# Output projections: the first token group stores its split weights to memory, and the later groups load them instead of splitting again

## The chip, the cores and the metric

The kernel runs on one core of one Trainium2 chip. The metric is the device time of one execution in microseconds (us). The engines are named as in the profile: PE (TensorE, matmuls), DVE (VectorE), ACT (ScalarE), POOL (GpSimd) and SP (SyncE, which here does little but issue transfers; SPq is its queue). "L298" is line 298 of the kernel.

## What is computed

The reference is a backbone of two layers over 1024 latent tokens and 256 context tokens, with a width of 1024. The change touches the last matrix product of each layer's token mixer, `@ w_out`:

```python
# layer 0 (mixer_ab): all 1024 latent tokens and the 256 context tokens
y_l = jnp.concatenate([a_l, b_l], axis=-1) @ w_out      # w_out: 1024 x 1024
y_c = jnp.concatenate([a_c, b_c], axis=-1) @ w_out
# layer 1 (mixer_cd): the latent tokens only, since the context is not needed behind the last layer
y_l = jnp.concatenate([c_l, d_l], axis=-1) @ w_out
...
xl = xl + ml[:, :, 2] * rms_norm(yl, g[1])
hl = modulate(rms_norm(xl, g[2]), ml[:, :, 3], ml[:, :, 4])
xl = xl + ml[:, :, 5] * rms_norm(conv_glu_ffn(hl, ...), g[3])
```

The products are made in float32 precision out of three faster ones: each operand is split into a rounded high part and a low remainder, and a product is high x high + low x high + high x low.

## The kernel before

**Tiles.** The tokens are worked in three groups: group 0 and group 1 of 512 latent tokens, and group 2, the context, of 256 (`TOK`). `outproj` (L588) makes one group's projection out of eight column tiles `o` of the weight, each 128 columns wide. For each tile `wcol` (L303) loads 128x8x128 floats of the weight (`wr`, 512 KB, L290), ACT rounds it to the high part `wh` (L295), and DVE or POOL subtracts to get the low part `wl` (L298): POOL throughout the projection of layer 0, DVE throughout that of layer 1. Then `gemm` issues 24 matmuls (L315 to L317: for each of 8 slices of the contraction one with `wh` and the input's high part, one with `wh` and its low part, one with `wl`). ACT copies the result out of the accumulator to `ys[o]` and squares it, and POOL adds the squares up (L472) for the norm.

Every group loads and splits the same eight tiles anew: three times in layer 0, twice in layer 1.

**Buffers.** `wr` has two buffers, so raw tiles are loaded ahead. `wh` and `wl` come from a pool `wgp` of two buffers each; in layer 0 every third tile goes to a third buffer in another pool (`third`, L302 to L306).

**What runs beside it.** `update` (L523) of a group starts when the group's projection is done, and works while the next one's matmuls run: it loads the residual x from memory (`xd`, L560), norms y (`rstd_y`: PE adds the squares over partitions at L436, `ones,sq`; DVE finds the reciprocal root in some twelve small steps at L439 to L444; DVE builds a diagonal matrix `dg` at L451, and PE spreads it at L456, `dg,ones`), adds y to x (DVE, L513 and L514), stores x (L547), squares it (ACT L468, POOL L472) and norms it for the FFN (DVE L495 and L498, ACT `hh`, POOL `hl` L502). `cat.load` of the next group loads and norms part of its input (`cln`, L812 to L841; its outputs are `cch` and `ccl`). After the projections the FFN starts: its first tile is two half tiles (`big`) for groups 0 and 1, and needs the normed x of both.

**What sets the order.** Instructions of an engine run in the order of its program. That order is made when the kernel is built, by flows that are advanced by estimated work (`pump`, and the numbers in `yield`), and then by a scheduler. All transfers of this stretch go through SP's queue in program order: a transfer that waits for a buffer or for data holds up all those behind it.

The same store and load of split weights is there already for another matrix: the FFN's down weights of layer 0 are stored to `wdd` (L1540) and loaded for the context (L1596).

Of the kernel before, what the change touches and what calls it, by code (L numbers as in the profile page):

```python
# [11 lines left out]
F32 = mybir.dt.float32  # L12
F32R = mybir.dt.float32r
# [60 lines left out]
PO1 = (), ("n+++++nn",)  # L74
PO0 = (), (), ()
# [15 lines left out]
OR0 = ()  # L91
GO0 = 0, 1, 2
YPO = 0, 1
U2 = 0, 1
PU1 = (), ("n+++++nn",)


@with_exitstack
def tile_backbone(ctx: ExitStack, tc: tile.TileContext, a: dict, out: bass.AP):
    nc = tc.nc  # L100
# [6 lines left out]
    wgp = ctx.enter_context(tc.tile_pool(name="wgp", bufs=2))  # L107
# [11 lines left out]
    drp = ctx.enter_context(tc.tile_pool(name="drp", bufs=1, space=DRAM))  # L119
# [3 lines left out]
    def nm(s):  # L123
        uid[0] += 1
        return f"{s}{uid[0]}"
# [5 lines left out]
    def psum_side(key, n):  # L131
        psy[0].close()
        psy[0] = ExitStack()
        psum[key] = psy[0].enter_context(tc.tile_pool(name=nm(key), bufs=n, space=PSUM))
# [8 lines left out]
    def page(shape, dt=F32, s="pg"):  # L143
        return pgp.tile(shape, dt, tag="pg", name=nm(s))
# [25 lines left out]
    def spawn(gen, key="norm"):  # L170
        flows.setdefault(key, deque()).append([gen, 0.0])
# [26 lines left out]
    def bank():  # L198
        return psum["mm"].tile([128, 512], F32, tag="mm", name=nm("mm"))
# [10 lines left out]
    def acts(g, n, dt=F32, s="act"):  # L210
        w = 2 if g < 2 else 4
        res = []
        for i in range(0, n, w):
            p = page([128, w, TOK[g]], dt, s)
            res += [p[:, j] for j in range(min(w, n - i))]
        return res
# [10 lines left out]
    def f32(ap):  # L227
        return ap.bitcast(F32)
# [59 lines left out]
    def load_w(src, nk, m=128):  # L288
        raw = rawp[0].tile([128, 8, 128], F32, tag="wr", name=nm("wr"), **({} if rawp[0] is wrp else {"bufs": 3}))
        nc.sync.dma_start(raw[:, 0:nk, 0:m], src)  # L290
        return raw

    def split_w(raw, nk=8, m=128, pages=False, pool=None, **kw):
        hi, lo = (page([128, 8, 128], F32R, x) if pages else (pool or wgp).tile([128, 8, 128], F32R, tag=x, name=nm(x), **kw) for x in ("wh", "wl"))
        S.copy(hi[:, 0:nk, 0:m], raw[:, 0:nk, 0:m])  # L295
        e = WS[ws[0]]
        wn[0] += 1
        (G if e[wn[0] % len(e)] == "G" else V).tensor_sub(lo[:, 0:nk, 0:m], raw[:, 0:nk, 0:m], f32(hi[:, 0:nk, 0:m]))  # L298
        return hi, lo
# [3 lines left out]
    def wcol(w, c0, m=128, pool=None, **kw):  # L303
        third[1] += 1
        if third[0] and third[1] % 3 == 0:
            pool, kw = ph[0], {"bufs": third[0]}  # L306
        nk = w.shape[0] // 128
        return split_w(load_w(w[:, c0:c0 + m].rearrange("(k p) m -> p k m", p=128), nk, m), nk, m, pool=pool, **kw)

    def gemm(ps, w, xh, xl, order=None):  # L310
        n = len(xh)
        order = order or range(n)
        for i, k in enumerate(order):
            wh, wl = w[0][:, k], w[1][:, k]
            T.matmul(ps, wh, xh[k], start=i == 0, stop=False)  # L315
            T.matmul(ps, wh, xl[k], start=False, stop=False)  # L316
            T.matmul(ps, wl, xh[k], start=False, stop=i == n - 1)  # L317
        pump(n * max(256, ps.shape[1]) / 800.0)
# [269 lines left out]
            pumping[0] = False  # L588
            return self[k]

    def outproj(w, cat, g, make, plan=lambda g: (), order=None):
        n = TOK[g]
        ys, sq = make(g), Sq(n, *plan(g))
        for o in range(8):
            wt = wcol(w, o * 128)
            ps = bank()[:, 0:n]
            gemm(ps, wt, *cat[g], order)
            last = S.copy(ys[o], ps)
            sq.add(ys[o])
        return ys, sq, last  # L600
# [7 lines left out]
    def mixer0(hs, nxt, xs0):  # L608
        w = a["ab_w_in"][0]
        pc = ph[0]  # L610
        rcos, rsin = pc.tile([128, 1024], F32, name="rcos", bufs=1), pc.tile([128, 1024], F32, name="rsin", bufs=1)
        protr = pc.tile([128, 3, 128], F32R, name="protr", bufs=1)
        with tc.tile_pool(name="m0a", bufs=1) as pa:
            prep = proj0(hs, w, pa, rcos, rsin, protr, xs0)
        psum_side("big", 2)
        cat = Lazy()
        with tc.tile_pool(name="m0b", bufs=1) as pb:
            attn0(pb, *prep, cat)
        ws[0] = "o0"
        with tc.tile_pool(name="m0o", bufs=8 * len(YPO)) as po:  # L620
            for i, g in enumerate(GO0):
                if i < 2:
                    spawn(cat.load(GO0[i + 1]), "cat")
                ys, sq, last = outproj(a["ab_w_out"][0], cat, g, (lambda g: [po.tile([128, 512], F32, tag="y", name=nm("y")) for _ in range(8)]) if g in YPO else (lambda g: acts(g, 8, F32, "y")), lambda g: PO0[g], range(7, -1, -1) if g in OR0 else None)
                drain("cat")
                spawn(update(0, g, ys, sq, 2, last, True, (0, 3, 4) if g < 2 else None, nxt, PU0[g]))
            pumping[0] = True
            while not posted >= {(0, g) for g in YPO}:
                advance(flows["norm"])
            pumping[0] = False  # L630
# [435 lines left out]
    def mixer1(hs, nxt):  # L1066
        pc = ph[0]
        w = a["cd_w_in"][0]
        tab = pc.tile([128, 1024], F32, name="tab", bufs=1)
        nc.scalar.dma_start(tab[64:96], a["rope2_s"][64:96])  # L1070
        nc.scalar.dma_start(tab[96:128], a["rope2_c"][96:128])
        KR = pc.tile([128, 1280], F32, name="kr", bufs=1)
        G.memset(KR[64:128], 0.0)
        G.memset(KR[96:97, 0:SEQ], -1.0)
        wv = []
        psum_side("ca", 1)
        with tc.tile_pool(name="m1a", bufs=1) as pa:
            proj1(hs, w, pa, tab, KR, wv)
        with tc.tile_pool(name="m1b", bufs=1) as pb:
            cat = mla(pb, tab, KR, wv)  # L1080
        ws[0] = "o1"
        with tc.tile_pool(name="m1o", bufs=8) as po:
            for g in range(2):
                if g < 1:
                    spawn(cat.load(1), "cat")
                ys, sq, last = outproj(a["cd_w_out"][0], cat, g, lambda g: acts(g, 8, F32, "y") if g else [po.tile([128, 512], F32, tag="y", name=nm("y")) for _ in range(8)], lambda g: PO1[g])
                drain("cat")
                spawn(update(1, g, ys, sq, 2, last, True, (1, 3, 4), nxt, PU1[g]))
            pumping[0] = True
            while (1, 0) not in posted:  # L1090
                advance(flows["norm"])
            pumping[0] = False
# [375 lines left out]
    def ffn(l, zp, hs, gs, early=None, done=None, tail=None):  # L1468
# [147 lines left out]
        for n_ in GRPS:  # L1616
            j0, j1 = j1, j1 + n_
            for j in range(j0, j1):
                if ctxp or j > 1 or not U2[l]:
                    up(j)  # L1620
# [205 lines left out]
```

## Time and profile before

| | |
|---|---|
| time, median of 3 runs | 3106.39 us (3103.65 to 3106.47) |
| the profiled execution's own time | 3102.78 us |
| its span, first to last instruction | 3101.0 us |
| mean granted clock of PE | 0.974 |
| PE busy | 2935.7 us (95%) |
| DVE, ACT, POOL busy | 1770.8, 1093.9, 995.8 us |

The projection of layer 0 runs from 470 to 615 us of the span, that of layer 1 from 2236 to 2327. Group 0's part of layer 0 ends at 518, group 1's at 580; the context follows until 614.5, and then the FFN. "Idle" in a row stands in square brackets, with the engine and the instruction that ended it.

### The profile page before, as it was taken

The numbers are of one execution on the slowest core, as the hardware profiler recorded it, in microseconds if no ns is written. First come the engines' busy times: TensorE is split into PE (matmuls) and PEld (weight loads), VectorE is DVE, ScalarE is ACT, GpSimd is POOL, SyncE is SP. The second block draws the span as 40 slices with busy tenths as digits, with TensorE's granted clock in tenths as the row PEclk, the third lists the DMA queues.
The fourth block names the chain that finished last, engine by engine and source line by source line (L and its number), as shares of the span: only waits on it lengthen the run. The fifth ranks groups of instructions, "written<-read, shape, count | busy, mean of one in ns | idle before, by whom it ended". The sixth has DMA issues, their size and how long they took to land. (4 is left out here: it accounts for less than half of the span.)

```text
span 3101.0 us, 37472 instructions
## 1 busy us (share of the span) xinstructions
PE 2935.7 (95%) x14441; PEld 2355.2 (76%) x14441; DVE 1770.8 (57%) x2631; ACT 1093.9 (35%) x1631; POOL 995.8 (32%) x730
## 2 busy tenths in 40 slices
PE   7997999899999999999999889999999999999998
PEld 4885777678888888879997556666677888888886
DVE  5899884664664455568545886676355132233234
ACT  5213884532121112144433763333444222111213
POOL 4676546820110001055432351110243222122223
PEclk8998999999999999999999999999998999999999
DMA  7443103433442344358744230010242121111212
GB/s 276 145 122 109 29 31 114 145 113 118 136 144 92 109 138 143 103 186 272 247 154 149 94 111 26 31 39 28 67 151 89 48 62 55 32 43 55 61 41 109
DMA packets 330769, 327.04 MB, mean 105 GB/s; under 512 B 27122, under 2 KB 280735, under 8 KB 330591
## 3 DMA queue, kind: packets, MB, share of 16 engines
q1 hardware_dynamic: 326784, 321.74, 32.3%
q10 hardware_dynamic: 3806, 2.91, 0.3%
q8 instruction: 113, 1.85, 0.2%
q14 instruction: 66, 0.53, 0.1%
HBM read 255.36 MB, written 69.21 MB: 105 GB/s over the span
## 5 line engine op out<-in xcount | busy, mean ns | idle before, releaser
L298 POOL TENSOR_TENSOR wl<-wr,wh 128x1024 fp32r<-128x1024 f32 x154 | 382.5, 2484 | 1301.1 <-ACT wh L295 1266.0
L295 ACT CAST wh<-wr 128x1024 fp32r<-128x1024 f32 x248 | 259.7, 1048 | 1067.0 <-PE big L316 666.8
L315 PE MATMUL big<-hh,wh 128*128 128x512 f32 x1376 | 540.6, 393 | 3.1 <-ACT hh L497 1.6
L316 PE MATMUL big<-hl,wh 128*128 128x512 f32 x1376 | 538.1, 392 | 1.5 <-POOL hl L502 1.4
L317 PE MATMUL big<-hh,wl 128*128 128x512 f32 x1376 | 537.7, 391 | 0.6 <-DVE wl L298 0.6
L315 PE MATMUL mm<-hh,wh 128*128 128x256 f32 (+1 forms) x1000 | 344.6, 345 | 10.0 <-DVE i L1030 9.5
L316 PE MATMUL mm<-hl,wh 128*128 128x256 f32 (+1 forms) x1000 | 337.8, 338 | 4.9 <-POOL hl L502 3.6
L317 PE MATMUL mm<-hh,wl 128*128 128x256 f32 (+1 forms) x1000 | 336.9, 337 | 5.1 <-DVE wl L298 3.0
L315 PEld LDWEIGHTS big<-hh,wh 128*128 128x128 f32 x1376 | 259.9, 189 | 59.0 <-ACT hh L497 3.4
L316 PEld LDWEIGHTS big<-hl,wh 128*128 128x128 f32 x1376 | 259.9, 189 | 57.3 <-POOL hl L502 3.8
L317 PEld LDWEIGHTS big<-hh,wl 128*128 128x128 f32 x1376 | 259.9, 189 | 55.1 <-DVE wl L298 1.0
L1552 PE MATMUL mm<-zh,wh 128*128 128x512 f32 x704 | 276.2, 393 | 1.2 <-ACT xt L1655 0.7
L1553 PE MATMUL mm<-zl,wh 128*128 128x512 f32 x704 | 274.5, 390 | 0.3 <-DVE zl L322 0.3
L1554 PE MATMUL mm<-zh,wl 128*128 128x512 f32 x704 | 274.5, 390 | 0.0
L472 POOL TENSOR_TENSOR sq<-t,sq 128x512 f32<-128x512 f32 (+1 forms) x153 | 196.6, 1287 | 177.5 <-ACT t L468 162.2
L1559 DVE TENSOR_TENSOR acc<-acc,mm 128x512 f32<-128x512 f32 x224 | 150.8, 685 | 175.1 <-PE mm L1554 174.7
L1484 DVE SCALAR_TENSOR_TENSOR ga<-big,C,ga 128x1023 f32<-128x1023 f32 x86 | 110.2, 1281 | 235.0 <-ACT ga L1497 233.6
L315 PEld LDWEIGHTS mm<-hh,wh 128*128 128x128 f32 x1000 | 191.5, 192 | 36.0 <-DVE i L1030 9.9
L316 PEld LDWEIGHTS mm<-hl,wh 128*128 128x128 f32 x1000 | 191.3, 191 | 29.2 <-POOL hl L502 6.4
L317 PEld LDWEIGHTS mm<-hh,wl 128*128 128x128 f32 x1000 | 191.2, 191 | 25.8 <-DVE wl L298 3.5
L298 DVE TENSOR_TENSOR wl<-wr,wh 128x1024 fp32r<-128x1024 f32 x94 | 137.1, 1459 | 110.4 <-ACT wh L295 106.9
L398 DVE SCALAR_TENSOR_TENSOR wa<-wm,sc,wa 128x256 f32<-128x256 f32 x280 | 146.6, 548 | 88.1 <-DMA wm<-in_w_mod_dram 85.6
(350 smaller groups left out, 5307.3 us busy)
## 6 DMA issues: line engine op xcount, KB each, us to landing
wr<-in_ffn_w_up_dram SPq DMA_DIRECT2D x132, 512.0 KB, 4.7
wm<-in_w_mod_dram SPq DMA_DIRECT2D x224, 128.0 KB, 2.2
wr<-in_ffn_w_down_dram SPq DMA_DIRECT2D x44, 512.0 KB, 3.6
wm<-in_w_mod_dram SPq DMA_DIRECT2D x40, 512.0 KB, 6.3
xd<-x SPq DMA_DIRECT2D x38, 512.0 KB, 4.6
x<-xd SPq DMA_DIRECT2D x38, 512.0 KB, 6.9
wr<-in_ab_w_out_dram SPq DMA_DIRECT2D x24, 512.0 KB, 7.7
wdd<-wh SPq DMA_DIRECT2D x22, 512.0 KB, 2.6
```

The costliest lines, as they stand in the source:

```text
L295: S.copy(hi[:, 0:nk, 0:m], raw[:, 0:nk, 0:m])
L298: (G if e[wn[0] % len(e)] == "G" else V).tensor_sub(lo[:, 0:nk, 0:m], raw[:, 0:nk, 0:m], f32(hi[:, 0:nk, 0:m]))
L315: T.matmul(ps, wh, xh[k], start=i == 0, stop=False)
L316: T.matmul(ps, wh, xl[k], start=False, stop=False)
L317: T.matmul(ps, wl, xh[k], start=False, stop=i == n - 1)
L398: V.scalar_tensor_tensor(acc[:, v], raw, sc[:, k, v:v + 1], acc[:, v], ALU.mult, ALU.add)
L472: self.eng.tensor_add(self.acc[-1], t, self.acc[-1])
L1484: V.scalar_tensor_tensor(dst[:, lo:hi], src[:, lo + d - o:hi + d - o], k, dst[:, lo:hi], ALU.mult, ALU.add)
L1552: T.matmul(ps, wh, zh, start=j == j0, stop=False)
L1553: T.matmul(ps, wh, zl, start=False, stop=False)
L1554: T.matmul(ps, wl, zh, start=False, stop=j == j1 - 1)
L1559: V.tensor_add(ys[g][c], ys[g][c], ps)
```

## The change

A tensor in device memory, `wod[l]`, holds the split tiles of each layer's weight. The first group splits each tile as before and also stores `wh` and `wl` (512 KB each; 16 stores for each layer). Later groups load both parts of a tile in `KEPT0` or `KEPT1` from there: in layer 0 all 8 tiles of group 1 and tiles 0, 2, 4 and 6 of the context, in layer 1 all 8 of group 1. For these 20 tiles there is no `wr`, no rounding on ACT and no subtraction (12 on POOL, 8 on DVE). Their `wh` and `wl` always come from the two buffers of `wgp`. Transfers on SP's queue go from 891 to 943: 32 stores and 40 loads come, 20 loads go.

```diff
+KEPT0 = (), tuple(range(8)), (0, 2, 4, 6)
+KEPT1 = (), tuple(range(8))
...
-    def outproj(w, cat, g, make, plan=lambda g: (), order=None):
+
+    wod = [drp.tile([8, 2, 128, 8, 128], F32, name=f"wod{l}") for l in range(2)]
+
+    def outproj(l, w, cat, g, make, plan=lambda g: (), order=None, first=False, kept=()):
         n = TOK[g]
         ys, sq = make(g), Sq(n, *plan(g))
         for o in range(8):
-            wt = wcol(w, o * 128)
+            if o in kept:
+                wt = [wgp.tile([128, 8, 128], F32R, tag=x, name=nm(x)) for x in ("wh", "wl")]
+                for q in range(2):
+                    nc.sync.dma_start(f32(wt[q]), wod[l][o, q])
+            else:
+                wt = wcol(w, o * 128)
+                if first:
+                    for q in range(2):
+                        nc.sync.dma_start(wod[l][o, q], f32(wt[q]))
             ps = bank()[:, 0:n]
             gemm(ps, wt, *cat[g], order)
```

The two calls of `outproj` pass `0, ..., i == 0, KEPT0[i]` and `1, ..., None, g == 0, KEPT1[g]`. Lines behind L95 move by 2, and those behind `outproj` by 13.

The scheduler orders other work anew around it. SP's queue in layer 0, from the end of group 0 into group 1, before; `wr` are raw tiles, `x<-xd` and `xd<-x` the residual's loads and stores, `cln` the context's input:

```order
134 L290 DMA wr_5011<-in_ab_w_out_dram 128x8x128
135 L290 DMA wr_5103<-in_ab_w_out_dram 128x8x128
136 L290 DMA wr_5155<-in_ab_w_out_dram 128x8x128
137 L560 DMA x_4976<-xd_103 128x1024
138 L560 DMA x_4977<-xd_103 128x1024
139 L560 DMA x_4978<-xd_103 128x1024
140 L560 DMA x_4979<-xd_103 128x1024
141 L812 DMA cln_5003<-cd_108 128x256 x4
142 L290 DMA wr_5190<-in_ab_w_out_dram 128x8x128
143 L290 DMA wr_5242<-in_ab_w_out_dram 128x8x128
144 L290 DMA wr_5296<-in_ab_w_out_dram 128x8x128
145 L547 DMA xd_103<-x_4976 128x1024
```

The same place now; `wh_5027` and `wl_5028` are tile 1 of group 1, `wh_5117` and `wl_5118` tile 2, `wh_5167` tile 3:

```order
154 L603 DMA wh_5027<-wod_106 128x1024
155 L562 DMA x_4992<-xd_103 128x1024
156 L562 DMA x_4993<-xd_103 128x1024
157 L562 DMA x_4994<-xd_103 128x1024
158 L562 DMA x_4995<-xd_103 128x1024
159 L825 DMA cln_5019<-cd_110 128x256 x4
160 L603 DMA wl_5028<-wod_106 128x1024
161 L603 DMA wh_5117<-wod_106 128x1024
162 L549 DMA xd_103<-x_4992 128x1024
163 L603 DMA wl_5118<-wod_106 128x1024
164 L549 DMA xd_103<-x_4993 128x1024
165 L549 DMA xd_103<-x_4994 128x1024
```

A tile's two halves now stand on both sides of the residual's transfers, and the loads for tiles 2 and 3 behind stores that wait for DVE's additions.

PE at the start of the FFN of layer 0, before: 24 matmuls of the first half tile with group 0 (`big_5816`), then the squares of group 1's new x (`ones,sq_5601`), 12 matmuls of the second half tile (`big_5817`), and the norm `dg_5872`; after that the two half tiles alternate to their common end.

```order
2237 L317 MATMUL mm_5764<-cah_2468,wl_5761 128x256
2238 L315 MATMUL big_5816<-hh_5329,wh_5806 128x512
...
2261 L317 MATMUL big_5816<-hh_5332,wl_5807 128x512
2262 L436 MATMUL mm_5855<-ones,sq_5601 128x1 x4
2263 L315 MATMUL big_5817<-hh_5329,wh_5812 128x512
...
2274 L317 MATMUL big_5817<-hh_5330,wl_5813 128x512
2275 L456 MATMUL mm_5874<-dg_5872,ones 128x512
2276 L315 MATMUL big_5817<-hh_5331,wh_5812 128x512
```

The same place now, with the names `sq_5599`, `dg_5866`, `big_5810` and `big_5811` for the same things:

```order
2235 L319 MATMUL mm_5758<-cah_2470,wl_5755 128x256
2236 L438 MATMUL mm_5849<-ones,sq_5599 128x1 x4
2237 L317 MATMUL big_5810<-hh_5333,wh_5800 128x512
2238 L318 MATMUL big_5810<-hl_5337,wh_5800 128x512
2239 L458 MATMUL mm_5868<-dg_5866,ones 128x512
2240 L317 MATMUL big_5811<-hh_5333,wh_5806 128x512
2241 L319 MATMUL big_5810<-hh_5333,wl_5801 128x512
```

The squares stand ahead of the FFN's first matmul, the norm two matmuls behind them; after these rows come the first half tile with both groups and only then, but for one matmul, the second. In the same way `dg` of group 0 stands behind two matmuls of group 1's tile 1 now, where it stood behind all 24.

## Rows read from the trace of the kernel before

**Rows 1.** The page: span, and the group of POOL's subtractions.

```profile
span 3101.0 us, 37472 instructions
L298 POOL TENSOR_TENSOR wl<-wr,wh 128x1024 fp32r<-128x1024 f32 x154 | 382.5, 2484 | 1301.1 <-ACT wh L295 1266.0
```

**Rows 2.** Windows: busy time of the engines in stretches of layer 0.

```profile
core 0: us, PE busy (x) PEld busy (x) DVE busy (x) ACT busy (x) POOL busy (x), PEclk, DMA share, GB/s
519.00:530.00 11.00, 11.00 (x54) 9.23 (x53) 4.72 (x12) 3.43 (x6) 6.05 (x3) 1.00 1.01 320
519.00:586.00 67.00, 53.18 (x217) 42.03 (x215) 48.78 (x78) 32.24 (x54) 46.07 (x26) 0.90 0.47 146
615.00:650.00 35.00, 29.98 (x120) 23.01 (x121) 21.52 (x33) 16.93 (x27) 19.91 (x15) 0.90 0.35 120
650.00:700.00 50.00, 50.00 (x226) 41.57 (x225) 37.92 (x75) 14.53 (x15) 5.28 (x3) 1.00 0.41 133
```

**Rows 3.** Timeline of PE, layer 0: start, duration, and idle before in brackets.

```profile
538.73 1.19 PE L821 MATMUL mm<-tot,ones 128*128 128x256 f32 x2 [2.30 <-DVE tot L818]
556.15 1.01 PE L436 MATMUL mm<-ones,sq 128*128 128x1 f32 x4 [4.24 <-DVE sq L472]
557.59 0.63 PE L316 MATMUL mm<-ccl,wh 128*128 128x512 f32 x1
563.30 0.39 PE L316 MATMUL mm<-cal,wh 128*128 128x512 f32 x1
572.42 1.53 PE L456 MATMUL mm<-dg,ones 128*128 128x512 f32 x4 [0.73 <-DVE dg L451]
586.12 0.58 PE L315 MATMUL mm<-cch,wh 128*128 128x256 f32 x1 [6.66 <-ACT cch L840]
624.46 1.87 PE L436 MATMUL mm<-ones,sq 128*128 128x1 f32 x8 [2.94 <-POOL sq L472]
631.13 1.02 PE L456 MATMUL mm<-dg,ones 128*128 128x512 f32 x2
649.48 0.47 PE L315 MATMUL big<-hh,wh 128*128 128x512 f32 x1 [1.09 <-DVE ga L1484]
```

**Rows 4.** Timeline of DVE, layer 0.

```profile
524.71 2.40 DVE L440 TENSOR_SCALAR rst<-rst 128x4 int32<-128x4 int32 x1
602.19 1.41 DVE L513 SCALAR_TENSOR_TENSOR t<-y,MOD,mm 128x512 f32<-128x512 f32 x2 [4.98 <-PE mm L456]
618.58 1.02 DVE L514 TENSOR_TENSOR x<-x,t 128x512 f32<-128x512 f32 x1
626.57 0.17 DVE L440 TENSOR_SCALAR rst<-rst 128x4 int32<-128x4 int32 x1
```

**Rows 5.** Timeline of POOL, layer 0.

```profile
524.66 2.42 POOL L298 TENSOR_TENSOR wl<-wr,wh 128x1024 fp32r<-128x1024 f32 x1 [1.80 <-ACT wh L295]
```

**Rows 6.** Timeline of SP's queue, layer 0.

```profile
517.67 2.17 SPq L560 DMA_DIRECT2D x<-xd  x4
519.88 3.82 SPq L812 DMA_DIRECT2D cln<-cd  x4
536.44 4.81 SPq L547 DMA_DIRECT2D xd<-x  x2
```

**Rows 7.** Transfers: KB each, median us from issue to landing (whole span, then 1550 to 1575 us).

```profile
x<-xd SPq DMA_DIRECT2D x38, 512.0 KB, 6.9
wdd<-wl SPq DMA_DIRECT2D x22, 512.0 KB, 3.0
wl<-wdd SPq DMA_DIRECT2D x22, 512.0 KB, 5.5
...
wh<-wdd SPq DMA_DIRECT2D x3, 512.0 KB, 3.7
```

**Rows 8.** Timeline of PE, layer 1: the one long wait of its projection.

```profile
2319.87 1.67 PE L456 MATMUL mm<-dg,ones 128*128 128x512 f32 x2 [4.66 <-DVE dg L451]
```

More of the change, by code (lines that the diff above doesn't have):

```diff
@@ L623, in mixer0 @@
                     spawn(cat.load(GO0[i + 1]), "cat")
-                ys, sq, last = outproj(a["ab_w_out"][0], cat, g, (lambda g: [po.tile([128, 512], F32, tag="y", name=nm("y")) for _ in range(8)]) if g in YPO else (lambda g: acts(g, 8, F32, "y")), lambda g: PO0[g], range(7, -1, -1) if g in OR0 else None)
+                ys, sq, last = outproj(0, a["ab_w_out"][0], cat, g, (lambda g: [po.tile([128, 512], F32, tag="y", name=nm("y")) for _ in range(8)]) if g in YPO else (lambda g: acts(g, 8, F32, "y")), lambda g: PO0[g], range(7, -1, -1) if g in OR0 else None, i == 0, KEPT0[i])
                 drain("cat")
@@ L1085, in mixer1 @@
                     spawn(cat.load(1), "cat")
-                ys, sq, last = outproj(a["cd_w_out"][0], cat, g, lambda g: acts(g, 8, F32, "y") if g else [po.tile([128, 512], F32, tag="y", name=nm("y")) for _ in range(8)], lambda g: PO1[g])
+                ys, sq, last = outproj(1, a["cd_w_out"][0], cat, g, lambda g: acts(g, 8, F32, "y") if g else [po.tile([128, 512], F32, tag="y", name=nm("y")) for _ in range(8)], lambda g: PO1[g], None, g == 0, KEPT1[g])
                 drain("cat")
```

## The prediction, made before the changed kernel was run

> **What bounds the kernel.** I read the page first. PE is busy for 95% of the span, so time is won or lost where PE stands idle or runs slowly, and nowhere else: the 20 roundings and subtractions that go are worth nothing by themselves. POOL's subtraction takes 2484 ns on average [rows 1], so 12 of them are 30 us of POOL, but POOL is not PE. The windows say where PE is short of work: in 519 to 586 us of layer 0 it is busy for 53.18 of 67 us, at a granted clock of 0.90, and in 615 to 650 for 29.98 of 35, again at 0.90; from 650 on it is busy for 50.00 of 50 [rows 2]. So a microsecond won before 650 stays won, and the change can touch little else there.
>
> The timeline of PE then names the waits of these stretches: 2.30, 4.24 and 0.73 us in group 1's projection, 6.66 ahead of the context, 2.94 for the squares of group 1's x, 1.09 for `ga` at the FFN's second tile [rows 3]. Behind a long wait PE also runs slowly. From 557.59 to 563.30 there are 15 matmuls in 5.71 us, 0.38 us each and at first 0.43; at full clock (226 in 50.00 us, rows of the last window) one takes 0.22 [rows 2, 3]. The first of them is a 0.63 us matmul, the last a 0.39 us one: the clock is at its lower level (1.2 GHz) after the 4.24 us pause and comes back to 2.4. That tail costs 5.71 - 15 x 0.22 = 2.4 us. I give a pause of 4 us or more 2.4 us beside its own length, and the 2.30 us one half of that.
>
> What made those waits? DVE's chain. One of its small steps takes 2.40 us at 524.71, where the same step takes 0.17 at 626.57 [rows 4], and it ends at 527.11, when POOL's subtraction that began at 524.66 ends (524.66 + 2.42 = 527.08) [rows 5]. A DVE step that meets a POOL subtraction waits it out. The Trainium skill says the same (SBUF — State Buffer, "Who interferes with whom": the port pair that VectorE and GpSimd share is an exclusive lock for a whole instruction), and the trace agrees, 2.40 against 0.17 us. So the removed subtractions do reach PE, by way of DVE.
>
> **The change, part by part.**
>
> *Stores of the first group.* 16 in each layer. A store of the same kind lands 3.0 us after its issue [rows 7], and a buffer is needed again only after its tile's 24 matmuls (24 x 0.22 = 5.4 us). They begin earlier than those matmuls end. Zero, with at most 1.5 us for a raw tile pushed back on SP's queue, in layer 1 above all, where loads of other tensors stand behind the stores. Without that cover each of 8 tiles would pay up to 3.0.
>
> *Removed waits, group 1 of layer 0.* 2.30 + 4.24 + 0.73 = 7.3 us of waiting, 1.2 + 2.4 = 3.6 of low clock: 10.9 together, if nothing else takes their place. Bounds: none of it (0) and all of it (10.9).
>
> *Late loads, group 1 of layer 0.* A kept tile can't be loaded until the tile two before it has freed its buffer; a raw tile was fetched further ahead. So the load is on the path now. Tile 0 of group 1 is early enough, since its buffer is free one tile before. Tile 1 is not: `wl_5028` stands in SP's order behind four loads of x and four of `cln`. Before, these were issued from 517.67 to 519.84 and 519.88 to 523.70 [rows 6], while the DMA engines moved 320 GB/s at a share of 1.01 [rows 2]. With `wh_5027` ahead, 3.5 MB (four of 0.5 for x, 0.5 for `cln`, two of 0.5 for the tile) have to be moved from 518.5 on: 11 us at 320 GB/s, so `wl_5028` lands near 529.5, and PE wants it behind tile 0 and the squares, 518.0 + 5.4 + 0.9 = 524.3. That is 5 us (if the larger pieces move faster, 3.5: from 524 by the 3.7 us of an undisturbed load [rows 7]), and its low clock 2.4. Tiles 2 and 3 stand behind stores of x that wait for DVE's additions; from 536.44 on before [rows 6], 1 or 2 us earlier now. A store, then 3.7 to 5.5 us for the load [rows 7]: I take 1.5 us each, between 0 and 3. Tiles 4 to 7 find an empty queue: two issues and 3.7 to 5.5 us against a cover of 5.4 make 0 to 1 each; I take 0. Sum 5 + 2.4 + 3 = 10.4. The pauses also overlap: while PE waits for tile 1, the load of tile 2 goes on. So I replay the stretch: tile 0 ends at 523.4, tile 1 at 529.5 + 5.4 + 2.4 = 537.3; then five tiles (27.0), one late load (1.5) and about 3 us of small matmuls of the norms lead to the pair of `dg` matmuls at 569, not 572.42 [rows 3]: -3. (The plain sum gives 10.4 - 10.9 = -0.5; I take the replay, since it lets pauses overlap.)
>
> *The context.* Its wait of 6.66 us [rows 3] stays, since `cch` comes out of the same chain behind `dg`; two subtractions less beside that chain shorten it by about 1.5. So the context starts 4.5 us earlier. Its tile 6 again stands behind stores of x, under a cover of half a tile: +2. After it -2.5.
>
> *The FFN's start.* Here the order of PE changes most. Before, PE ran 24 matmuls and waited 2.94 us at 624.46 for the squares of x [rows 3], which come after DVE's additions (602.19 to 619.60, 17.4 us [rows 4]). Now the squares stand ahead of all of them, so that PE waits for that chain with nothing in hand. The chain starts 4.5 us earlier (597.7), and the additions take about 14.5 us with half of POOL's subtractions gone; 3 us for the squares: 615, when PE has waited from 612. The norm then takes what it took from 624.46 to 631.13 less the matmuls between, about 5.6 us [rows 3]. Behind it stand 94 matmuls at 0.22, 2.4 us of low clock and 1 of small ones: 620.6 + 24.3 = 645 for the second tile, which starts at 649.48 before [rows 3]; it no longer waits for `ga` (1.09), since the half tiles follow one another. So -4.5; between -8 (chain 3 us faster) and 0.
>
> *Layer 1.* The same trade on a smaller scale: the one long wait, 4.66 us [rows 8], and its low clock go, since DVE loses its own 8 subtractions; tile 1's pair stands behind 3 MB of other loads, about 4.2 us and low clock. -0.5, between -5 and +5.
>
> *Elsewhere* the scheduler moves a few operations in other stages; 0, plus or minus 2.
>
> **Sum.** -4.5 - 0.5 = -5 us on the profiled execution's 3102.78. That execution is 3.6 us below the median of the runs; I take the difference against the median, 3106.39 - 5 = 3101.
>
> One more figure stands by itself: the Trainium skill (DMA: Bandwidth & Descriptors, "Where 436 GB/s comes from") limits memory traffic of one core to about 358 GB/s, by which a pair of 1 MB would take 2.9 us and, with its fixed 2.0 us, 4.9: an estimate inside a tile, by which the sum would stay as it is. The trace has 320 GB/s in a full stretch.
>
> **Rivals.**
>
> *The loads don't keep up (slower).* Every kept tile has two buffers, so its load runs under one tile's matmuls, 5.4 us. In the whole span such a load lands 5.5 us after issue, and x, in heavier traffic, 6.9 [rows 7]; with two issues of half a us each that is 6.5 to 7.9. PE then waits 1.1 to 2.5 us at every other tile at least, and with traffic at every tile: over the 14 tiles behind the first of each group 8 to 20 us. From the forecast that is +3 to +15; I put it at +9, 3115. For it: kept tiles move 8 MB for a group where raw ones moved 4, in stretches where the engines were full. Against: 3.7 us undisturbed. It decides from a landing of about 4.4 us.
>
> *Nothing is late (faster by more).* If tile 1's pair lands by 526 and the stores of x don't hold up tiles 2 and 3, the 10.9 us come in whole and layer 1 gains its 4.66: -13, 3093.
>
> *It cancels.* The late loads take all that POOL gives, the FFN's start waits for the same chain: -1 to +3, 3107. A change that does nothing is no rival: POOL's 12 subtractions are surely gone.
>
> **Chances.** What a measurement tells from no change is 0.2%, 6.2 us. The forecast, -9 to -1: 0.54, its faster end (beyond -6.2) 0.25 of it. More gain 0.16. Cancelled 0.12. Slower 0.18, all but a little beyond +6.2. That makes faster 0.41, same 0.42, slower 0.17. The range leaves a tenth on either side: 3090 (-16) to 3114 (+8). The forecast's own range is 3097 to 3105.
>
> **What would show it.** Right: POOL's `wl` rows gone from 520 to 586; the step that took 2.40 us near 0.2; PE's waits of 2.30 and 4.24 replaced by one for a transfer of `wl` ahead of tile 1; the pair of `dg` near 569, the context near 581, the FFN's second tile near 645; layer 1 within 5 us. Wrong: waits for `wh` or `wl` transfers at tiles 4 to 7, or the squares ahead of the FFN's first matmul later than 618.

## The result: slower by 0.5%, and the profile after

The changed kernel takes 3119.27 us, median of 4 runs (3116.43 to 3122.20), beside 3105.02 for the kernel before (3100.61 to 3106.47): a ratio of 1.0052, 95% interval 1.0040 to 1.0064. Forecast were 3101 and a range of 3090 to 3114. Slower had been given a chance of 0.17, by another mechanism than the one that was found.

The profiled execution took 3122.20 us, its span is 3120.1 (before 3101.0 [rows 1]). The page of the changed kernel; the last row answers to POOL's in [rows 1]. The 12 subtractions are gone.

```profile
span 3120.1 us, 37523 instructions
L300 POOL TENSOR_TENSOR wl<-wr,wh 128x1024 fp32r<-128x1024 f32 x142 | 353.6, 2491 | 1296.6 <-ACT wh L297 1269.8
```

Windows of the changed kernel, columns as in [rows 2]; the second row answers to the row of the same stretch there.

```profile
519.00:530.00 11.00, 8.54 (x42) 6.75 (x40) 2.48 (x12) 2.44 (x4) 1.74 (x2) 1.00 0.94 306
519.00:586.00 67.00, 53.07 (x227) 41.56 (x225) 38.33 (x78) 26.47 (x48) 27.21 (x20) 0.92 0.61 214
586.00:622.00 36.00, 29.64 (x200) 28.41 (x201) 15.86 (x28) 13.12 (x26) 22.57 (x19) 0.82 0.66 230
```

In group 1 of layer 0 POOL's busy time falls from 46.07 to 27.21 us and DVE's from 48.78 to 38.33, and PE, which they were to help, does 227 operations where it did 217. In the context (586 to 622) PE is busy for 29.64 of 36 us at a clock of 0.82. The kernel before took from 586 to 615 for it, at a clock of 0.94:

```profile
586.00:615.00 29.00, 27.07 (x203) 25.69 (x203) 16.34 (x26) 14.49 (x27) 24.79 (x17) 0.94 0.59 185
```

There the loss begins.

To see where time goes I compared start times of the same PE rows in both traces, and took the distance between two such rows for each stretch, so that what came earlier drops out. The stretches are: **group 1 of layer 0**, from the squares of group 0 (`ones,sq`, 523.53 us before) to the pair of `dg` matmuls (572.42 [rows 3]); **context and FFN start**, from that pair to the context's `dg` in the FFN (676.76); **first group of layer 1**, from the row in which PE waits for the last slice of its input (`ch`, 2236.51) to its squares (2279.64), which stand behind tile 0 of group 1; **behind it**, from there to the last pair of `dg` matmuls in layer 1's FFN (2368.07).

Each stretch holds the same number of matmuls in all kernels of this document (168, 468, 174 and 334), so the distances can be compared. They are taken between starts rounded to 0.1 us and can be off by as much. The projection of layer 1 does not start at 2236, as stated above: PE has worked on tiles 0 and 1 since 2225.75, and the third stretch leaves that part out. The first group of layer 0, which also stores, lies ahead of the first stretch. From its first matmul to its squares it takes 53.7 us before (469.79 to 523.53) and in the changed kernel (471.76 to 525.50).

```
us                      group 1   context and   first group   behind
                        layer 0   FFN start     layer 1       it
before                  48.9      104.3         43.1          88.5
changed                 46.3      111.1         48.8          93.8
difference              -2.6      +6.8          +5.7          +5.3
```

Sum +15.2 of the span's +19.1; the other 3.9 lie elsewhere (2.0 of them ahead of layer 0's projection).

**Group 1 of layer 0.** Timeline of PE, changed kernel; the rows answer to 538.73, 556.15 and 572.42 in [rows 3].

```profile
529.49 1.22 PE L458 MATMUL mm<-dg,ones 128*128 128x512 f32 x2 [2.46 <-DVE dg L453]
533.88 0.79 PE L319 MATMUL mm<-cch,wl 128*128 128x512 f32 x1 [3.17 <-DMA wl<-wod]
547.77 0.47 PE L317 MATMUL mm<-cch,wh 128*128 128x512 f32 x1 [1.20 <-DMA wh<-wod]
559.49 0.50 PE L438 MATMUL mm<-ones,sq 128*128 128x1 f32 x4
571.83 1.45 PE L458 MATMUL mm<-dg,ones 128*128 128x512 f32 x4
```

The waits of 2.30, 4.24 and 0.73 us have gone. In their place PE waits 2.46 for `dg` and 3.17 for a load, 5.6 together, in tile 1 (`dg` stands behind two of its matmuls now, and the load goes on while PE waits for it), and 1.20 ahead of tile 3. The queue shows why. SP's queue, changed kernel:

```profile
520.03 0.32 SPq L603 DMA_DIRECT2D wh<-wod  x1
520.40 1.91 SPq L562 DMA_DIRECT2D x<-xd  x4
522.36 3.61 SPq L825 DMA_DIRECT2D cln<-cd  x4
527.29 0.32 SPq L603 DMA_DIRECT2D wl<-wod  x1
```

The low part is issued 7.3 us after the high part. Timeline of DVE, changed kernel; the first row answers to the step of 2.40 us at 524.71 in [rows 4], the second makes the squares that PE waited 4.24 us for at 556.15 in [rows 3]:

```profile
526.68 0.17 DVE L442 TENSOR_SCALAR rst<-rst 128x4 int32<-128x4 int32 x1
547.97 2.37 DVE L474 TENSOR_TENSOR sq<-t,sq 128x256 f32<-128x256 f32 x3
```

The squares are ready at 550.34, 9.1 us before PE comes to them at 559.49. With no subtraction on POOL beside it, the small step takes 0.17 us. That is what the Trainium skill (SBUF — State Buffer, "Who interferes with whom") would have; the trace agrees.

**The context.** Timeline of PE, changed kernel; the first row answers to 586.12 in [rows 3], the last two to 624.46 and 631.13.

```profile
585.40 0.58 PE L317 MATMUL mm<-cch,wh 128*128 128x256 f32 x1 [6.64 <-ACT cch L853]
597.66 0.39 PE L319 MATMUL mm<-cch,wl 128*128 128x256 f32 x1 [1.04 <-DMA wl<-wod]
610.85 0.35 PE L317 MATMUL mm<-cch,wh 128*128 128x256 f32 x1 [1.52 <-DMA wh<-wod]
615.09 0.58 PE L319 MATMUL mm<-cch,wl 128*128 128x256 f32 x1 [3.54 <-POOL wl L300]
622.21 0.95 PE L438 MATMUL mm<-ones,sq 128*128 128x1 f32 x8
629.11 2.08 PE L458 MATMUL mm<-dg,ones 128*128 128x512 f32 x2 [3.99 <-DVE dg L453]
```

From the context's first matmul to the squares behind it, 36.8 us (585.40 to 622.21). Before, the eight tiles took from 586.12 to the FFN's first matmul at 614.93: 28.8. So the context costs 8.0 more, and only part of that is a wait for a load: the longest is for POOL. SP's queue there, and then ACT's and POOL's rows for the tile behind, in the changed kernel:

```profile
606.33 0.32 SPq L549 DMA_DIRECT2D xd<-x  x1
606.75 0.37 SPq L603 DMA_DIRECT2D wh<-wod  x1
609.42 0.32 SPq L549 DMA_DIRECT2D xd<-x  x1
609.84 0.37 SPq L603 DMA_DIRECT2D wl<-wod  x1
```

```profile
609.29 1.05 ACT L297 CAST wh<-wr 128x1024 fp32r<-128x1024 f32 x1 [0.93 <-PE mm L318]
612.25 2.79 POOL L300 TENSOR_TENSOR wl<-wr,wh 128x1024 fp32r<-128x1024 f32 x1
```

The two halves of the context's tile 6 are each issued behind a store of x that waits for DVE's additions, and the split of the computed tile 7 comes so late that PE stands until 615.04 (612.25 + 2.79), and then works at the lower clock. Its rounding had to wait until PE was done with the high part of the tile two before.

**The first group of layer 1**, which only stores. Timelines of PE, then ACT, then SP's queue, changed kernel:

```profile
2264.30 0.79 PE L317 MATMUL mm<-ch,wh 128*128 128x512 f32 x1 [4.16 <-ACT wh L297]
2298.38 0.71 PE L317 MATMUL mm<-ch,wh 128*128 128x512 f32 x1 [4.00 <-DMA wh<-wod]
2348.99 0.50 PE L318 MATMUL big<-hl,wh 128*128 128x512 f32 x1 [3.10 <-POOL hl L504]
```

```profile
2263.20 1.04 ACT L297 CAST wh<-wr 128x1024 fp32r<-128x1024 f32 x1 [2.44 <-DMA wr<-in_cd_w_out_dram]
```

```profile
2250.00 2.81 SPq L1466 DMA_DIRECT2D t<-attd  x3
2252.86 0.42 SPq L608 DMA_DIRECT2D wod<-wl  x1
2253.34 0.42 SPq L608 DMA_DIRECT2D wod<-wh  x1
2254.83 0.32 SPq L608 DMA_DIRECT2D wod<-wl  x1
2255.19 2.57 SPq L292 DMA_DIRECT2D wr<-in_cd_w_out_dram  x2
```

PE waits 4.16 us for a rounding on ACT, ACT waits for its raw tile, and the raw tile was issued at 2255.19 behind three stores, the last of them of a low part that DVE had just made. But the place in the queue need not be all. Windows of the changed kernel: from the issue of the raw tiles to their rounding, and the first group of layer 0.

```profile
2255.00:2263.00 8.00, 5.14 (x22) 3.90 (x22) 0.00 (x0) 2.33 (x4) 5.93 (x5) 1.00 0.96 313
471.76:525.50 53.74, 53.01 (x239) 42.55 (x238) 17.10 (x29) 23.02 (x35) 29.69 (x18) 1.00 0.61 198
```

While ACT waits, the DMA engines are busy for 0.96 of the time, so the bytes of the stores may delay the raw tiles as much as the place in the queue does. In layer 0's first group, where they are busy for 0.61, raw tiles are issued behind stores too (one at 499.46, behind the store of a low part at 499.05), and the group takes no longer than before. The 4.66 us wait for `dg` [rows 8] is gone, and 4.00 for tile 1 have come. The FFN then begins with a wait of 3.10 us for `hl`.

### The profile page after: what moved, and what is told of

It reads as the page before. It is cut to its first block, busy times and chain, and to the rows that moved or that the text cites. A ratio compares the mean times of both kernels' runs of the same rounds, so it can differ in the third digit from the quotient of the medians.

```text
span 3120.1 us, 37523 instructions
## 1 busy us (share of the span) xinstructions
PE 2941.1 (94%) x14441; PEld 2357.3 (76%) x14441; DVE 1741.3 (56%) x2623; ACT 1076.7 (35%) x1611; POOL 962.4 (31%) x718
## 5 line engine op out<-in xcount | busy, mean ns | idle before, releaser
L300 POOL TENSOR_TENSOR wl<-wr,wh 128x1024 fp32r<-128x1024 f32 x142 | 353.6, 2491 | 1296.6 <-ACT wh L297 1269.8
L297 ACT CAST wh<-wr 128x1024 fp32r<-128x1024 f32 x228 | 238.8, 1048 | 1037.4 <-PE big L318 681.4
L300 DVE TENSOR_TENSOR wl<-wr,wh 128x1024 fp32r<-128x1024 f32 x86 | 124.4, 1447 | 100.5 <-ACT wh L297 100.4
```

## The experiments

Times are medians beside the kernel before on the same chip. For the first four rows of the table below that is 3104.18 us (27 runs), for the next four 3104.34 (23), for the last four 3102.79 (26). All stretches, as in the table above:

```
us                           group 1   context and   first group   behind
                             layer 0   FFN start     layer 1       it
stores only                  49.0      104.6         47.9          87.6
layer 0 alone                46.6      110.3         44.1          87.5
layer 1 alone                49.0      104.5         47.1          91.4
one load a group             44.3      101.0         49.3          81.9
stores on ACT's queue        47.0      113.2         52.8          89.4
loads on ACT's queue         48.6      109.9         55.0          88.0
layer 0, group 1 alone       47.0      105.6         43.3          89.0
layer 0, third buffer        44.1      101.2         44.1          87.8
layer 1, late stores         49.0      104.4         46.4          91.7
layer 1, stores on POOL's    48.7      104.1         46.1          89.5
third buffer, group 1 alone  44.9      103.9         43.6          87.5
third buffer, context whole  43.9      103.1         43.4          88.3
```

Stretches that a kernel doesn't change lie within 0.3 and 0.5 us of each other in layer 0, within 1.0 us in the first group of layer 1 and 1.5 us behind it (43.1 to 44.1 and 87.5 to 89.0 for the kernels without the change there). But the table holds one execution of each kernel, the profiled one, and that can lie off the median: 4.8 us below it for layer 1 alone, 10.6 above it for the loads on ACT's queue. The changed kernel and layer 1 alone have the same layer 1 and differ there by 1.7 and 2.4 us. So I take a difference of 2 us for one in layer 0, and of 3 in layer 1.

**Stores only.**

```diff
-KEPT0 = (), tuple(range(8)), (0, 2, 4, 6)
-KEPT1 = (), tuple(range(8))
+KEPT0 = (), (), ()
+KEPT1 = (), ()
```

> The first groups of both layers store their split tiles, and no later group loads them: all groups split as before. Theory Q (the queue: in the changed kernel's trace a raw tile of layer 1's first group is issued behind the stores at 2255.19 us, and PE waits 4.16 us for its rounding): layer 1's first group loses about 5 us here too, layer 0's nothing, so 4 to 7 us above the kernel before. Rival L (the loads alone cost): within 2 us of the kernel before.

3108.98 us, ratio 1.0013 (1.0003 to 1.0023), 4 to 5 us up. Layer 0 is unchanged (49.0 and 104.6), layer 1's first group takes 47.9 for 43.1. The first group of layer 0 takes 53.7 us here too. So the stores of layer 1 cost 4 to 5 us by themselves, those of layer 0 nothing.

**Layer 0 alone, and layer 1 alone.** The other layer's `first` is set to `False` and its `KEPT` to empty.

> The change in layer 0 alone; layer 1 as before. By the two traces compared event by event, the stretch from the first projection of layer 0 to the second tile of the FFN is 4 us longer, and the other stretches up to layer 1 move by plus 2 to plus 4: 3 to 8 us above the kernel before. Theory Q puts the loss into the context (8 us, two late tiles), with a gain of 3 to 4 in group 1. Rival P (the prediction was right for layer 0, and what the profiled execution shows there is scatter): 3 to 6 us below the kernel before.

> The change in layer 1 alone; layer 0 as before. By the two traces layer 1's projection and the start of its FFN are 11 us longer (5 in the first group, 6 behind it): 9 to 12 us above the kernel before. If the loss of both layers adds up, this and the run with layer 0 alone make together the 14 us of the whole change. Rival (the loss comes from the order of work in other stages, which the scheduler makes anew for any edit): below 5 us.

Layer 0 alone 3109.36, ratio 1.0016 (1.0007 to 1.0024); layer 1 alone 3114.40, ratio 1.0035 (1.0023 to 1.0048). Over the kernel before that is 5.2 and 10.2, together 15.4; the whole change gave 14.3. The losses add up, so the two layers can be looked at apart. In the table layer 1 alone loses only 6.9 (4.0 and 2.9) and not 10.2, since its profiled execution, 3109.56 us, is its fastest.

**One load a group.**

```diff
-            if o in kept:
+            if o in kept and o:
+                pass
+            elif o in kept:
                 wt = [wgp.tile([128, 8, 128], F32R, tag=x, name=nm(x)) for x in ("wh", "wl")]
```

> As the changed kernel, but of the kept tiles only tile 0 of each group is loaded, and all kept tiles of the group use it: it leaves out the loads of the other kept tiles (18 of 20), so its output is not the projection. It shows what the removed splitting is worth when no kept load can be late; the stores stay. Theory Q: the waits for kept loads (6 to 9 us in each layer with their low clock) go, the 5 us of layer 1's stores stay: 8 to 14 us below the changed kernel, 0 to 4 above or below the kernel before. Rival D (the removed splitting is worth what the waits of before add up to, 10.9 in layer 0 and 7 in layer 1): 10 to 15 us below the kernel before.

3096.28, ratio 0.9975 (0.9965 to 0.9985): 7.9 us below the kernel before, some 22 below the changed one. It fell between the two theories. The removed splitting is worth something: 4.6 us in group 1 of layer 0, 3.3 behind it, 6.6 in layer 1's group 1, 14.5 in all, of which the stores of layer 1 take 6.2 back (49.3 for 43.1). It isn't the 10.9 and 7 that the removed waits add up to. In group 1 of layer 0 PE still waits here:

```profile
536.30 0.67 PE L836 MATMUL mm<-tot,ones 128*128 128x256 f32 x2 [0.70 <-DVE tot L833]
551.72 1.02 PE L438 MATMUL mm<-ones,sq 128*128 128x1 f32 x4 [3.82 <-DVE sq L474]
```

The 2.30 us wait shrinks to 0.70, but the one of 4.24 stays at 3.82 with no subtraction left to stretch DVE's steps: the squares come earlier, 29.0 us behind those of group 0 for 32.6 before, and so does PE. In the changed kernel the wait was gone, since DVE made these squares earlier still, 24.8 us behind those of group 0 (550.34); why is open.

**Stores on ACT's queue, loads on ACT's queue.** `nc.scalar.dma_start` for `nc.sync.dma_start`, at the stores or at the loads.

> The changed kernel with its 32 stores issued on ACT's queue and not on SP's; the 40 kept loads stay on SP's. Theory Q (raw tiles of layer 1's first group wait on SP's queue behind stores, which wait for DVE): the 5 to 6 us of layer 1's first group come back, 4 to 7 us below the changed kernel, about 8 to 10 above the kernel before. Rival W (it is the bytes: the memory's time for 1.5 MB a tile, whatever the queue): no better than the changed kernel, about 15 above.

> The changed kernel with its 40 kept loads issued on ACT's queue and not on SP's; the stores stay on SP's. Theory Q: kept loads no longer stand behind x loads, x stores and the FFN's raw tiles, so tile 1 of both layers and the context's tile 6 come earlier: 5 to 9 us below the changed kernel. Rival T (two buffers and the landing time set it): the waits for kept tiles stay, within 2 us of the changed kernel. Rival A (a load that waits on ACT's queue holds up ACT's copies and squares, so that DVE's chains come later): above the changed kernel.

Stores there 3122.74, ratio 1.0065 (1.0052 to 1.0077); loads there 3117.23, ratio 1.0041 (1.0026 to 1.0056). Over the kernel before that is 18.4 and 12.9. Both expectations of theory Q failed, and the times are those of the rivals: no better than the changed kernel with the stores there (W), within 2 us of it with the loads there (T). The stores on ACT's queue made the first group of layer 1 longer (52.8) and not shorter. With the loads there, what is behind layer 1's first group comes down to 88.0 as before the change, but the first group goes to 55.0, in an execution far above the median. That ACT is held up by transfers that wait on its queue (A) is shown once, with the stores there: a rounding waits 1.70 us behind the store of a low part that DVE has still to make. The longest waits for a rounding, 3.23 and 2.90 us of PE, come from elsewhere: ACT waits for the attention's parts (`t<-attd`) ahead of the one, and for a raw tile ahead of the other. Another queue is no free place, and these runs don't exclude the bytes as the cause.

**Layer 0, group 1 alone.** As layer 0 alone, with `KEPT0 = (), tuple(range(8)), ()`.

> The change in group 1 of layer 0 alone: the context splits all its tiles as before, layer 1 is as before. Theory Q: group 1 gains 2 to 3 us at its pair of norm matmuls, as in the changed kernel, and the context's 8 us of late tiles go: 5 to 8 us below the run with layer 0's change whole, 0 to 3 below the kernel before. Rival: the context was not the loss, the order at the start of the FFN was: as the run with layer 0's change whole, about 5 above the kernel before.

3104.72, ratio 1.0001 (0.9993 to 1.0010). Without the kept context tiles the loss behind group 1 goes from 6.0 to 1.3 us, and the gain of group 1 (1.9) is about taken back. That is 4.8 us below the run with layer 0's change whole, and 0.4 above the kernel before where theory Q had 0 to 3 below. The context's kept tiles were the loss of layer 0.

**Layer 0 with the third buffer.** The kernel before had sent every third split tile of layer 0 to a third buffer; the change had kept tiles always use two. This run gives it back:

```diff
-                wt = [wgp.tile([128, 8, 128], F32R, tag=x, name=nm(x)) for x in ("wh", "wl")]
+                third[1] += 1
+                pool, kw = (ph[0], {"bufs": third[0]}) if third[0] and third[1] % 3 == 0 else (wgp, {})
+                wt = [pool.tile([128, 8, 128], F32R, tag=x, name=nm(x), **kw) for x in ("wh", "wl")]
```

> The change in layer 0 alone, with every third tile, a kept one too, in the third buffer that the kernel before used for split tiles. Then a kept load runs under two tiles' matmuls (11 us) at a third of the tiles, and the loads of tile 1 of group 1 stand ahead of the loads of x on SP's queue. Theory T (two buffers leave a load no slack): the wait ahead of tile 1 and the late tiles of the context go, 4 to 8 us below the run with layer 0's change whole, 0 to 4 below the kernel before. Rival: the waits move on to tile 2, whose low part now stands behind the loads of x: within 2 us of the run with layer 0's change whole.

3098.02, ratio 0.9986 (0.9975 to 0.9996): 6.3 us below the kernel before, 11.5 below the same change with two buffers, more than theory T had. The two stretches of layer 0 take 44.1 and 101.2, as much as with one load a group (44.3 and 101.0): with three buffers the loads of layer 0 cost nothing more. SP's queue in this run:

```profile
509.25 0.32 SPq L605 DMA_DIRECT2D wh<-wod  x1
509.67 0.38 SPq L605 DMA_DIRECT2D wl<-wod  x1
514.69 0.32 SPq L605 DMA_DIRECT2D wh<-wod  x1
515.06 1.85 SPq L562 DMA_DIRECT2D x<-xd  x4
517.01 2.74 SPq L827 DMA_DIRECT2D cln<-cd  x4
520.72 0.32 SPq L605 DMA_DIRECT2D wl<-wod  x1
```

And the timeline of PE:

```profile
549.19 1.02 PE L438 MATMUL mm<-ones,sq 128*128 128x1 f32 x4 [3.78 <-DVE sq L474]
577.46 0.58 PE L317 MATMUL mm<-cch,wh 128*128 128x256 f32 x1 [6.18 <-ACT cch L855]
600.65 0.39 PE L319 MATMUL mm<-cch,wl 128*128 128x256 f32 x1 [1.18 <-DMA wl<-wod]
638.18 0.47 PE L317 MATMUL big<-hh,wh 128*128 128x512 f32 x1 [1.09 <-DVE ga L1499]
```

Tile 1's two halves are issued together at 509.25, ahead of x; it is tile 2's low part now that stands behind x and `cln`, and it is needed a tile later. No wait for a load is left in group 1, one of 1.18 in the context. The order of PE at the FFN's start is the old one again (`ga` ends the wait ahead of the second tile), so buffer and order changed together here, and I can't give each its share.

**Layer 1, stores written one tile later, and stores on POOL's queue.** Both on the run with layer 1 alone.

```diff
+        def put():
+            while due:
+                p, t = due.pop()
+                for q in range(2):
+                    nc.sync.dma_start(wod[l][p, q], f32(t[q]))
...
+                put()
                 if first:
-                    for q in range(2):
-                        nc.sync.dma_start(wod[l][o, q], f32(wt[q]))
+                    due.append((o, wt))
...
```

> The change in layer 1 alone (11 us above the kernel before in its first form), with each tile's stores written in the program one tile later, so that on SP's queue the raw load of the next tile but one stands ahead of more of them. Theory Q (the first group of layer 1 loses 5 us because a raw load is queued behind four stores): the wait of 1.6 to 4.2 us for a rounding in the first group goes, 3 to 5 us below the first form, 6 to 8 above the kernel before. Rival W (bytes: the memory can't move two stores, a raw tile and the attention's parts in a tile's time): within 2 us of the first form.

> The change in layer 1 alone, with the 16 stores issued on POOL's queue. Theory Q: no raw load waits behind a store on SP's queue any more; 3 to 6 us below the first form (11 above the kernel before). Rival W (bytes): within 2 us of it. Rival B (the queue's engine is held up, as ACT was in the run with the stores there): above the first form, since POOL makes the low parts of the attention's output in that stretch.

3112.68, ratio 1.0027 (1.0017 to 1.0038), and 3110.70, ratio 1.0025 (1.0014 to 1.0035), beside 1.0035 for the first form: the intervals overlap, so the times don't decide. Nor do the stretches: 46.4 and 46.1 for 47.1. The traces say a little more. PE's waits for a rounding in the first group add up to 1.0 us with late stores and to none with the stores on POOL's queue, for 2.1 in the first form (4.6 in the changed kernel). But tile 0 of group 1, which lies ahead of the end of the stretch, now waits for its load, 2.3 us with the stores on POOL's queue, and with late stores:

```profile
2277.83 0.50 PE L319 MATMUL mm<-ch,wl 128*128 128x512 f32 x1 [1.73 <-DMA wl<-wod]
```

So moving the stores does what theory Q says to the raw tiles, and the kept loads take the time instead. Rival W, the bytes, would have it so too, and isn't excluded. Nor is the wait the whole loss: in the first form PE waits only 0.8 us more than before in this stretch, in all, and the rest of its 4.0 us are slow matmuls:

```profile
2240.00:2245.00 5.00, 5.00 (x12) 3.94 (x13) 0.89 (x1) 4.05 (x8) 4.83 (x5) 0.50 0.76 257
```

The granted clock is 0.50 there, the lower level, behind three short waits of PE (1.46, 0.62 and 0.43 us between 2234 and 2239); over the stretch it is 0.93, for 1.00 before.

**Third buffer: group 1 alone, and the context whole.**

> The change in group 1 of layer 0 alone (0.4 above the kernel before with two buffers), with the third buffer for every third tile. Theory T (the gain of 4.5 us at group 1's pair of norm matmuls is there once a kept load has room, and the context neither gains nor loses): 3 to 6 us below the kernel before, and about 2 to 3 above the run with the third buffer and half of the context kept, where the context and the start of the FFN gain 3 too. Rival (the gain with the third buffer comes from the context): within 2 us of the kernel before.

> The change in layer 0 alone with the third buffer, and all 8 tiles of the context kept, not 4. A context tile is 24 matmuls of 256 columns, 2.9 us, so even two tiles' cover, 5.8 us, is about what a pair of loads takes (3.7 us to 9 in this stretch). Theory T: the context is late by 5 to 10 us, so 0 to 5 above the kernel before. Rival R (relief of DVE and POOL is what counts, and the loads have room): another 2 to 4 us below the run with half of the context kept (which was 6 below the kernel before).

Group 1 alone 3098.93, ratio 0.9990 (0.9981 to 0.9999); context whole 3102.16, ratio 0.9997 (0.9987 to 1.0007). Group 1 alone has most of the gain (44.9 for 48.9), 3.9 us below the kernel before, as theory T expected. With all eight tiles kept, the context and the FFN's start take 103.1, 1.9 more than with four. T had that in sign but not in size: the run is 0.6 below the kernel before, where T had 0 to 5 above. By the intervals the three kernels with the third buffer don't differ.

## Why the prediction was wrong, step by step

**Stores of the first group: wrong in layer 1.** They were put at "zero, with at most 1.5 us for a raw tile pushed back on SP's queue". In layer 0 that held (first group 53.7 us with the stores and without). In layer 1 they measured 4.8 (47.9 for 43.1) and 5.7 in the changed kernel. The raw tile pushed back, which the step priced at 1.5 at most, is what came: the one long wait for its rounding is 3.16 us with the stores only and 4.16 in the changed kernel, and matmuls run slowly behind it. The step counted a store by itself, with 3.0 us to land; here several stores and the attention's loads share the DMA engines (0.96 busy). Whether the place in the queue or the bytes delay the raw tile more, no run shows.

**Late loads and removed waits in group 1 of layer 0: the sum right, by luck.** The pair of `dg` came 46.3 us behind the squares and not 48.9, -2.6 for -3. Tile 1's pause was 5.6 us for 5 (2.46 of it under the wait for `dg`), with low clock behind it. But both halves were too large, and cancelled: without late loads the gain is 4.6, not 10.9, since 3.82 of the 4.24 us stay there, and against that run the late loads cost 2.0 and not 7.9.

**The context: wrong, the largest term of layer 0.** It was to start 4.5 us earlier and lose 2; it started about 2.6 earlier by the stretch before it and lost 8.0. I counted tile 6's load alone, and its wait is 1.52. What stands behind it is the split of a computed tile, whose rounding needs a buffer that PE has just given up; PE waits 3.54 for it, and such pauses bring their own low clock (0.82 in that window, 0.94 before). So the sign of being wrong came, squares later than 618: they stand at 622.21.

**The FFN's start: right behind the norm, not ahead of it.** From `dg` (629.11) to the second tile (653.41) it is 24.3 us, which is what was worked out (645 - 620.6). From the squares to `dg` it is 6.9, for 5.6 (by its own words, 6.67 less twelve matmuls of 0.22, that term was 4.0). The wait for the squares with nothing in hand, from 612 to 615, did not come: PE reaches them at 622.21 without a wait, because the context was late. So the second tile starts 3.9 us later than before (2.0 of it from ahead of the projection), and not 4.5 earlier.

**Layer 1 behind the first group: wrong by 6.** Forecast -0.5, measured +5.3. The wait of 4.66 did go, and 4.00 for tile 1 came (forecast 4.2); most of the rest lies at the start of the FFN, from its first matmul to the last `dg` 44.3 us for 40.1. PE waits there 3.10 to 3.12 us for `hl` in all six kernels that load every kept tile of layer 1, 1.52 with one load a group and 0.44 with the stores only. Timelines of ACT and of SP's queue, changed kernel:

```profile
2343.76 1.05 ACT L297 CAST wh<-wr 128x1024 fp32r<-128x1024 f32 x1 [1.73 <-DMA wr<-in_ffn_w_up_dram]
2340.09 7.58 SPq L292 DMA_DIRECT2D wr<-in_ffn_w_up_dram  x2
```

Ahead of the `hh` that `hl` is made from, ACT stands for a raw tile of the FFN, 1.73 to 2.05 us in the six kernels. It is issued when POOL's subtraction has freed its buffer, 2.8 us ahead of the FFN's first matmul (2342.90); before, it was issued 9.4 us ahead (2318.51 for 2327.93). The 4.66 us wait and the slow matmuls behind it had left time for the FFN's first splits. Without that wait PE comes to the FFN 6.3 us behind `dg` and not 8.1, and waits there instead. The prediction had the wait that goes, and not the one behind it. This is read from the traces; no run separates it.

**Elsewhere: plus or minus 2.** 3.9 in the profiled execution. In stretches that no edit touches the same distance varies by 1 us, and the start of layer 0's projection by five from kernel to kernel (466.4 to 471.8), so I don't read more into it.

**The rivals.** "The loads don't keep up" had the right sign and nearly the right price (+9 forecast, +14 measured), but not the mechanism: steady landing times were to exceed 5.4 us of cover in group 1's tiles 4 to 7, and in the changed kernel no wait for a load stands there in layer 0, and one of 0.71 us (tile 4) in layer 1. The long waits stand at tile 1 of both layers and in the context. At tile 1 of layer 1 the high part is issued at 2289.03 and takes 9.2 us to land. In layer 0 they stand where SP's queue holds a transfer behind others, and with the third buffer one of 1.18 us is left. "Nothing is late" is what one load a group shows: -7.9 us with layer 1's stores still in it, not -13.

## What to carry to other kernels

Replacing a recomputation by a load moves the work from an engine with slack to an ordered queue, and the time then depends on what stands ahead in that queue: count, for each new store and load, which transfer behind it is needed next, for which data the one ahead of it waits, and how busy the DMA engines are there already. A load that replaces a split made from a prefetched tile may need a buffer more than the split did; with the buffer the same change in layer 0 went from 5 us slower to 6 us faster. Layer 1, which has two thirds of the loss, was not run with a third buffer. And a wait that adds up in the profile is not the gain of removing one of its causes: leave the work out in a run of its own first, with nothing in its place, and see what is there to win.

## What was not expected of the hardware

In the first group of layer 1 the transfers come in bursts. The changed kernel's transfers from 2240 to 2300 us, in 40 slices of 1.5 us:

```profile
DMA  0397268757998992299999908897179999999999
GB/s 30 107 321 265 78 202 339 238 191 239 414 410 247 279 294 53 116 401 396 388 200 338 254 10 347 355 396 287 33 218 414 326 305 296 388 377 399 418 423 418
```

Slices of 10 and 33 GB/s stand beside slices of 418 and 423. The gaps are not where the raw tile was late: from 2255 to 2262 the DMA engines' busy share is 0.8 and above in each slice, while the rate falls from 414 to 247 GB/s and rises to 294. The Trainium skill (DMA: Bandwidth & Descriptors, "Where 436 GB/s comes from") puts the limit of one core's memory traffic at about 358 GB/s, as half of what two cores share, and names beside it 425 GB/s measured with a transfer of 16 MB. Only one core runs here. The trace doesn't agree with the first figure: the last three slices, 4.5 us, are above 410.
